# Chunked attention scores: the low-half pass of the queries over all 128 rows

## Chip, cores and metric

The kernel runs on one NeuronCore of a Trainium2 chip. The metric is device time in microseconds (us) of one execution, as the median of several runs. The engines are named as in the profile: PE is TensorE (PEld its weight loads), DVE is VectorE, ACT is ScalarE, POOL is GpSimd, SP is SyncE, which issues the DMAs here.

## The reference

One encoder layer on 1024 positions and 1024 channels in float32:

```
mod   = silu(c) @ w_ada + b_ada                     # six rows of shift, scale, gate
h     = rmsnorm(x) * (1 + scale) + shift
proj  = h @ w_in                                    # latents, rotary key, q/k/v of the chunked heads
o_mla = latent attention   (8 heads, chunk-causal, 96 channels a head)
o_ca  = chunk_attention(rmsnorm(cq), rmsnorm(ck), cv, rel_bias)    # 8 heads of 64 channels
x     = x + g_a * (concat(o_mla, o_ca) @ w_out)
x     = x + g_m * (silu(gate) * val @ w_down)       # gate, val = causal conv of (h2 @ w_up)
```

In `chunk_attention` each chunk of 64 queries sees the keys of its own chunk and of the 8 chunks before it; the scores are scaled by 64 ** -0.5, a clipped relative-position bias is added, and a softmax follows. The change is in the product of queries and keys of these heads.

## The kernel before

**Precision.** Matmuls run on float32r operands. A float32 value is split into a high half (the value rounded to float32r) and a low half (what is left), and a product is the sum of high by high, high by low and low by high (`gemm3`, L151 to L156).

**Chunked heads.** Two heads (o = 0 and 1) share a page: rows 0 to 63 of a tile hold the 64 channels of the even head, rows 64 to 127 those of the odd one, and 512 positions lie along the columns. `ca_pages` makes the pages of a pair p (0 to 3) and a group g (0 or 1: the positions 0 to 511 or 512 to 1023). Four transposes on PE bring the normalized queries into PSUM (`page_psum`, L729). For each head, `qh[o]` holds the queries' high half twice: in the head's own rows (ACT, L755) and, copied by POOL (L757), in the other 64 rows. `kk[:, o]` holds the keys' high half in the head's own rows and their low half in the other rows (L761, L762). One matmul over 128 rows of `qh[o]` and `kk[:, o]` so gives high by high and high by low together. The queries' low half, `ql` (DVE, L756), is one tile for both heads, each head in its own 64 rows. The third product, low by high, is a second matmul over the head's own 64 rows alone.

**Score tiles.** A unit is one head of one group, with four tiles of 128 queries; `scores` (L797) runs the qh pass and then the ql pass into the same PSUM tile. Keys come in one segment for the tiles of group 0 (128 to 512 columns) and in two for those of group 1 (512 and 128, 384 and 256, and so on). After the scores, DVE adds the bias and takes the minimum (L818; the sign is turned, so that the minimum is what the softmax subtracts), ACT takes the exponential with its sum (L829), DVE the reciprocal (L831, L832), POOL and DVE write the probabilities as two float16 halves (L73, L851), SP transposes them by DMA (L863), and PE multiplies them by the values (L891). A unit's pages are made two tiles ahead of it.

**Latent heads.** They come after the chunked heads, with the same chain. Their queries' high and low halves have tiles of the tag Q2 too (`qk_page`), and their three score products run over 96 rows each (L803).

**Order.** The program is written as score tiles with filler work between them (`pace`): the other input projections (L154 to L156), the latents, the up projections. The order on each engine is planned at build time from priorities and data readiness; the scores have a higher priority than the fillers. A side job, `f_ada`, computes rows 2 to 4 of `mod`: 48 pieces of 128 by 512 of `w_ada` are loaded by SP (L446) and multiplied and summed on DVE (L458, L460), one step at a time among the fillers; each load is placed behind the SP instruction issued last, each step behind the last score minimum. The pieces, the running sum and later the raw tiles of `w_out` (`load_wo`, L699) share the buffers of the tag A.

**Memory.** A tag's `bufs` is the number of its tiles that exist at one time. `apg` and `at` are pools of the attention stage; `at` lies where the tiles of the starting stage lay.

Of the kernel before, what the change touches and what calls it, by code (L numbers as in the profile page):

```python
# [13 lines left out]
F32 = mybir.dt.float32  # L14
F32R = mybir.dt.float32r
# [7 lines left out]
MUL, ADD, SUB, MIN, MAX = ALU.mult, ALU.add, ALU.subtract, ALU.min, ALU.max  # L23

P = 128
# [39 lines left out]
def layer_kernel(ctx, tc, I, out):  # L65
    nc = tc.nc
    pe, act, dve, pool, sp = nc.tensor, nc.scalar, nc.vector, nc.gpsimd, nc.sync

    def f32(ap):
        return ap.bitcast(F32)  # L70
# [57 lines left out]
    apg = att_pg.__enter__()  # L128
# [13 lines left out]
        return apg.tile([P, 512], F32, name=name, tag="sq", bufs=2)  # L142

    def atile(name):
        return apg.tile([P, 512], F32, name=name, tag="A", bufs=5)

    def pgtile(shape, dt, name):
        return apg.tile(shape, dt, name=name, tag="pg", bufs=6)
# [133 lines left out]
    for d in range(ND):  # L282
        dd, half = divmod(d, 2)
# [6 lines left out]
        pt = ps.tile([P, 512], F32, name=f"p_ada{d}", tag="mm", bufs=2)  # L290
# [23 lines left out]
    at = att.__enter__()  # L314
# [121 lines left out]
    def f_ada():  # L436
        steps = [(m, n, k) for m in (2, 3, 4) for n in range(2) for k in range(ND)]
        wt = {}

        def load(i):  # L440
            if i < len(steps):
                m, n, k = steps[i]
                wt[i] = atile(f"aw{m}_{n}_{k}")
                c0 = m * D + n * 512
                with tc.issue_after(anchor["sp"]):
                    sp.dma_start(wt[i][:], I["w_ada"][k * P:(k + 1) * P, c0:c0 + 512])  # L446

        for i in range(3):
            load(i)
        yield 0  # L450
        yield 0
        for i, (m, n, k) in enumerate(steps):
            if k == 0:
                acc = atile(f"aacc{m}_{n}")
            load(i + 3)
            with tc.issue_after(anchor["dve"]):
                if k == 0:
                    dve.tensor_scalar(acc[:], wt[i][:], cs[:, 0:1], None, op0=MUL)  # L458
                else:
                    dve.scalar_tensor_tensor(acc[:], wt[i][:], cs[:, k:k + 1], acc[:], op0=MUL, op1=ADD)  # L460
            yield 0
            if k < ND - 1:
                continue
            yield 0
            pt = ps.tile([P, 512], F32, name=f"p_ada{m}_{n}", tag="mm", bufs=2)
            if m == 2:
                gate_bcast(pt[:], acc, m * D + n * 512, 512, qtile)
                g = qtile(f"gab{n}")
                act.activation(g[:], pt[:], AF.Copy)
                sp.dma_start(ga_d[:, n * 512:(n + 1) * 512], g[:])  # L470
            else:
                for j in range(4):
                    pe.matmul(pt[:, j:j + 1], acc[:, j * P:(j + 1) * P], ones[:, 0:1], start=True, stop=True)
                act.activation(modT[:, 3 if m == 3 else 2, 4 * n:4 * n + 4], pt[:, 0:4], AF.Copy)
            yield 0
        b = pk[:, C_B + 24:C_B + 40].rearrange("p (a b) -> p a b", a=2)
        dve.tensor_tensor(modT[:, 3, :], modT[:, 3, :], b[:, 0], op=ADD)
        dve.tensor_tensor(modT[:, 2, :], modT[:, 2, :], b[:, 1], op=ADD)
        dve.scalar_tensor_tensor(modT[:, 2, :], modT[:, 2, :], 1.0, pk[:, C_GM:C_GM + ND], op0=ADD, op1=MUL)
# [240 lines left out]


    def q2(name):
        return at.tile([P, 512], F32R, name=name, tag="Q2", bufs=6)

    def page_psum(src, name, rows, tag="T"):
        pt = ps.tile([P, 512], F32, name=f"{name}_ps", tag=tag, bufs=TB)
# [18 lines left out]
    def ca_pages(p, g):  # L745

        qn = qns[p, g]
        half = (slice(0, 64), slice(64, 128))
        pt = page_psum(lambda j: qn[:, j, 0:128], f"q{p}_{g}", P)
        if p == g == 0:  # L750
            pk_ = page_psum(lambda j: qn[:, j, 128:256], f"k{p}_{g}", P, "pv")
        qh = [q2(f"qh{p}_{g}_{o}") for o in range(2)]
        ql = q2(f"ql{p}_{g}")
        for o in range(2):
            act.activation(qh[o][half[o]], pt[half[o]], AF.Copy)  # L755
            dve.tensor_tensor(ql[half[o]], pt[half[o]], f32(qh[o][half[o]]), op=SUB)  # L756
            pool.tensor_copy(qh[o][half[1 - o]], f32(qh[o][half[o]]))  # L757
        pt = pk_ if p == g == 0 else page_psum(lambda j: qn[:, j, 128:256], f"k{p}_{g}", P)
        kk = at.tile([P, 2, 512], F32R, name=f"k{p}_{g}", tag="K", bufs=3)
        for o in range(2):  # L760
            act.activation(kk[half[o], o], pt[half[o]], AF.Copy, scale=gk_ca[half[o]])  # L761
            dve.scalar_tensor_tensor(kk[half[1 - o], o], pt[half[o]], gk_ca[half[o]], f32(kk[half[o], o]),  # L762
                                     op0=MUL, op1=SUB)
        return (qh, ql), kk

    class Unit:
# [7 lines left out]
        def scores(u, i):  # L774

            qpg, kpgs = u.pages()
            bias = u.bias() if u.band else None
            lo = max(0, i - 4) if u.band else 0
            n = (i - lo + 1) * P
# [3 lines left out]
            with tc.high_priority(offset=OFF_S):  # L783
                s = ps.tile([P, 1024], F32, name=f"s{nm}", tag="S", bufs=2)
                n0 = max(0, min(4, i + 1) - lo) * P
                n1 = n - n0
                c0 = 512 - n0 if n1 else 0
                segs = [(c0, lo * P, n0, 0)] if n0 else []
                if n1:
                    segs.append((512, max(lo, 4) * P - 512, n1, 1))  # L790
                q = slice((i % 4) * P, (i % 4 + 1) * P)
                rs_ = slice(u.base, u.base + u.rows)
                if u.band:
                    qh, ql = qpg
                    for a, rr in ((qh[u.odd], slice(0, P)), (ql, rs_)):
                        for c, ko, w, kh in segs:
                            last = pe.matmul(s[:, c:c + w], a[rr, q], kpgs[kh][rr, u.odd, ko:ko + w],  # L797
                                             start=(a is not ql), stop=(a is ql))
                else:
                    for a in range(2):  # L800
                        for c, ko, w, kh in segs:
                            for b in range(2 - a):
                                last = pe.matmul(s[:, c:c + w], qpg[a][rs_, q], kpgs[kh][rs_, b, ko:ko + w],  # L803
                                                 start=(a == 0 and b == 0), stop=(a == 1))
                trail.append(last.ins)
                sv = s[:, c0:c0 + n]
                m = cst.tile([P, 1], F32, name=f"m{nm}", tag="m", bufs=4)
                if u.band:
                    if i >= 4:
                        dve.memset(sv[64:128, 0:64], BIG)  # L810
                    w = min(n, 256)
                    if n > 256:
                        m0 = cst.tile([P, 1], F32, name=f"m0{nm}", tag="m0", bufs=4)
                        dve.tensor_reduce(m0[:], sv[:, :n - 256], axis=AX.X, op=MIN)
                        init = m0[:]
                    else:
                        init = 3e38
                    anchor["dve"] = dve.tensor_tensor_reduce(sv[:, n - w:n], sv[:, n - w:n], bias[:, 256 - w:256], 1.0, init,  # L818
                                             ADD, MIN, accum_out=m[:]).ins
                else:  # L820
                    dve.memset(sv[0:64, n - 64:n], BIG)
                    anchor["dve"] = dve.tensor_reduce(m[:], sv, axis=AX.X, op=MIN).ins  # L822
                short = n <= (640 if u.band else 512)
                pieces = [(0, n)] if short else [(0, 512), (512, n)]
                if n <= 640:
                    pr = at.tile([P, 640], F32, name=f"P{nm}", tag="P", bufs=P_BUFS)
                else:
                    pr = pgtile([P, 1024], F32, f"P{nm}")
                act.activation(pr[:, :n], sv, AF.Exp, bias=m[:], scale=-1.0, accum_out=rsum[:, 0:1])  # L829
            with tc.high_priority(offset=OFF_P):  # L830
                dve.reciprocal(ri[:], rsum[:, 0:1])  # L831
                dve.tensor_scalar(ri[:], ri[:], PSCALE, None, op0=MUL)  # L832
                for x, (p0, p1) in enumerate(pieces):
                    w = p1 - p0
# [33 lines left out]
        def values(u, i):  # L868
# [17 lines left out]
            with tc.high_priority(offset=OFF_V):  # L886
                for x, (_, j, c, w, mov) in enumerate(todo):
                    dst = u.pv[:, c:c + w]
                    if w > P:
                        dst = dst.rearrange("p (a b) -> p a b", a=2)  # L890
                    last = pe.matmul(dst, u.vst(j), mov, start=(x == 0), stop=(x == len(todo) - 1),  # L891
                                     skip_group_check=True)
                trail.append(last.ins)
                if i % 4 == 3:
# [9 lines left out]
                    else:  # L904
                        anchor["om"] = sp.dma_start(u.dst_d[r0, u.g * 512:(u.g + 1) * 512], dst[r0]).ins
            return 56 * sum(w // P for _, _, _, w, _ in todo)

    cnt = [0]
    pair = [0]
# [112 lines left out]
    for n in range(len(tiles) + DEPTH):  # L1022
        if n < len(tiles):
            u, i = tiles[n]
# [9 lines left out]
        if n >= DEPTH:  # L1034
            u, i = tiles[n - DEPTH]
# [140 lines left out]
    for t in range(NT):  # L1176
        pt = ps2.tile([P, 1024], F32, name=f"op{t}", tag="op", bufs=3)
# [36 lines left out]
    for k in range(4):  # L1214
# [4 lines left out]
        for q, wl, wh in rows0:  # L1219
            product(q[:, 512:], wl, "b12", add=k > 0, ks=[k], skip=True)  # L1220
            last = product(q[:, 512:], wh, "b22", add=True, ks=[k])
# [226 lines left out]
    def load(o, i):  # L1448
        inorder("sp", sp.dma_start, o, i)
# [199 lines left out]
```

## Time and profile before

| | |
|---|---|
| runs | 1331.33, 1333.23, 1334.52 us; median 1333.23 us |
| profiled execution, first to last instruction | 1332.7 us |
| mean granted PE clock | 0.958 |
| busy: PE, PEld, DVE, ACT, POOL | 91%, 75%, 82%, 47%, 43% |
| instructions | 18710 |

The profile lists no time of the profiled execution beside its span; the span is 0.5 us below the median of the runs. A busy PE is not a PE at its peak, since the ends of matmuls are modelled; the starts of matmuls and of weight loads are what the steps are read from. In a timeline row the columns are start, duration, engine, line, operation, tiles (out<-in), shape and count, and in brackets the idle time of that engine before it with what ended it; "issue" means that nothing which the profile shows was waited for. The shape of a PE row begins with rows*columns of the weights. The row of a stretch gives its length and, for each engine, busy time and instructions, then the granted clock, the DMA share and GB/s.

### The profile page before, as it was taken

Reading aid. Unit: us, or ns where it says so; the run is one execution under the profiler, and the core shown is the slowest. Engines: PE = TensorE matmul, PEld = TensorE weight load, DVE = VectorE, ACT = ScalarE, POOL = GpSimd, SP = SyncE. Lnnn points to the kernel's source line nnn. Section 1 sums busy time; section 2 is a strip of 40 time slices with the busy share of each in tenths; the row PEclk is TensorE's granted clock in tenths of the full one; section 3 lists DMA queues with packets and bytes.
Section 4 is the critical chain, followed back from the end, with each engine's and each line's share of the span. In section 5 each row is a group of like instructions: output and inputs, shape, how many; then the busy total and the mean of one; then the engine's idle time right before and its main releaser. Section 6 shows DMA issues by size and latency. Waiting matters only on the chain.

```text
span 1332.7 us, 18710 instructions
## 1 busy us (share of the span) xinstructions
PE 1212.8 (91%) x6168; PEld 997.1 (75%) x6168; DVE 1088.7 (82%) x1928; ACT 622.3 (47%) x1132; POOL 572.3 (43%) x610
## 2 busy tenths in 40 slices
PE   3899999989667798888889999999999998999998
PEld 3888878868555576666677888888888886888886
DVE  6979898877589967894779888898889986687667
ACT  5454654445555545553366444444443444443331
POOL 5476773675675633354615445444444541000000
PEclk9899999989878798997999999999999998999999
DMA  8416768766123685879702333333333336943441
GB/s 321 144 55 156 164 143 197 150 151 138 35 72 70 119 172 122 152 164 326 275 16 79 106 124 111 122 116 108 113 106 132 111 119 221 393 151 114 132 159 63
DMA packets 223689, 190.57 MB, mean 143 GB/s; under 512 B 148708, under 2 KB 166884, under 8 KB 223592
## 3 DMA queue, kind: packets, MB, share of 16 engines
q1 hardware_dynamic: 223592, 189.38, 50.3%
q8 instruction: 48, 0.79, 0.3%
q14 instruction: 49, 0.40, 0.1%
HBM read 117.24 MB, written 37.49 MB: 116 GB/s over the span
## 4 chain that ended last, share of the span: by engine, by line
PE 48%; DVE 3%; DMA 2%; issue 1%; ACT 1%; POOL 0%; SPq 0%; POOLq 0%; DVEq 0%
PE p L1125 10%; PE p L1126 10%; PE p L1127 10%; PE dnA_P L1460 2%; PE dnA_P L1461 2%; PE dnA_P L1462 2%; PE dnB_P L1461 1%; PE dnB_P L1460 1%; PE dnB_P L1462 1%; PE dnA L1461 1%; PE dnA L1460 1%; PE dnA L1462 1%; PE dnB L1461 1%; PE dnB L1462 1%; PE dnB L1460 1%
## 5 line engine op out<-in xcount | busy, mean ns | idle before, releaser
L77 ACT ACTIVATE dnP<-dnr 128x1024 fp32r<-128x1024 f32 x73 | 77.4, 1064 | 117.5 <-PE dnA_P L1462 46.4
L1434 DVE TENSOR_TENSOR dnP<-dnr,dnP 128x1024 fp32r<-128x1024 f32 x72 | 87.9, 1224 | 52.7 <-ACT dnP L77 47.7
L73 POOL TENSOR_SCALAR hlm<-Pm,rim 128x512 f16<-128x512 f32 (+2 forms) x96 | 65.4, 691 | 77.5 <-DVE rim L832 32.0
L84 POOL TENSOR_TENSOR wf<-wu,wf 128x512 fp32r<-128x512 f32 x22 | 39.8, 1808 | 118.2 <-ACT wf L77 118.2
L1296 DVE SCALAR_TENSOR_TENSOR u<-c,cvp,u 128x1023 f32<-128x1023 f32 x44 | 58.6, 1372 | 27.8 <-ACT u L1295 27.8
L84 POOL TENSOR_TENSOR wb<-wu,wb 128x512 fp32r<-128x512 f32 x22 | 42.2, 1920 | 75.0 <-ACT wb L77 59.6
L73 POOL TENSOR_SCALAR hlc<-Pc,ric 128x640 f16<-128x640 f32 (+2 forms) x64 | 48.0, 753 | 54.5 <-DVE ric L832 25.8
L851 DVE SCALAR_TENSOR_TENSOR hlm<-Pm,rim,hlm 128x512 f16<-128x512 f32 (+2 forms) x96 | 65.9, 696 | 5.5 <-POOL hlm L73 5.2
L829 ACT ACTIVATE Pc<-sc,mc 128x640 f32<-128x640 f32 (+2 forms) x64 | 42.2, 660 | 55.2 <-DVE mc L818 26.1
L891 PE MATMUL pvm<-PTm,vt 128*128 128x256 f16 (+1 forms) x320 | 47.7, 302 | 22.1 <-DMA PTm<-hlm 14.2
L829 ACT ACTIVATE Pm<-sm,mm 128x128 f32<-128x128 f32 (+3 forms) x64 | 47.1, 738 | 37.7 <-DVE mm L822 21.2
L1295 ACT ACTIVATE u<-c,cvp 128x1024 f32<-128x1024 f32 x44 | 52.4, 1238 | 26.0 <-DVE c L1394 18.0
L1297 DVE SCALAR_TENSOR_TENSOR u<-c,cvp,u 128x1022 f32<-128x1022 f32 x44 | 61.7, 1442 | 0.0
L891 PEld LDWEIGHTS <-vt 128*128 128x128 f16 x320 | 33.1, 111 | 37.0 <-issue 21.6
L77 ACT ACTIVATE wc<-ws 128x512 fp32r<-128x512 f32 x21 | 13.3, 632 | 91.9 <-DVE ws L1144 86.1
L154 PE MATMUL ipq<-wq_s,hT 128*128 128x256 f32 x192 | 55.7, 290 | 0.0
L156 PE MATMUL ipq<-wq_s,hT 128*128 128x256 f32 x192 | 55.4, 288 | 0.0
L155 PE MATMUL ipq<-wq_s,hT 128*128 128x256 f32 x192 | 55.1, 287 | 0.0
L851 DVE SCALAR_TENSOR_TENSOR hlc<-Pc,ric,hlc 128x640 f16<-128x640 f32 (+2 forms) x64 | 49.2, 774 | 6.8 <-POOL hlc L73 6.7
L1461 PE MATMUL dnA_P<-dnP 128*128 128x512 f32 x132 | 51.3, 389 | 0.0
L1462 PE MATMUL dnA_P<-dnP 128*128 128x512 f32 x132 | 51.3, 389 | 0.0
L1460 PE MATMUL dnA_P<-dnP 128*128 128x512 f32 x132 | 51.2, 389 | 0.0
(442 smaller groups left out, 4413.7 us busy)
## 6 DMA issues: line engine op xcount, KB each, us to landing
wu<-w_up SPq DMA_DIRECT2D x44, 512.0 KB, 3.5
dnr<-g_d SPq DMA_DIRECT2D x73, 256.0 KB, 2.8
aw<-w_ada SPq DMA_DIRECT2D x48, 256.0 KB, 3.4
g_d<-u SPq DMA_DIRECT2D x22, 512.0 KB, 3.0
dnr<-w_down SPq DMA_DIRECT2D x44, 256.0 KB, 5.4
adaw<-w_ada_a SPq DMA_DIRECT2D x16, 512.0 KB, 6.0
x<-x SPq DMA_DIRECT2D x16, 512.0 KB, 9.8
g_d<-gs SPq DMA_DIRECT2D x22, 256.0 KB, 2.8
```

Source lines behind the costliest of these rows:

```text
L73: pool.tensor_scalar(o, i, s, 1.0, op0=MUL, op1=MUL)
L77: act.activation(o, i, AF.Copy)
L84: (pool if eng == "p" else dve).tensor_tensor(o, i, f32(hi), op=SUB)
L829: act.activation(pr[:, :n], sv, AF.Exp, bias=m[:], scale=-1.0, accum_out=rsum[:, 0:1])
L851: dve.scalar_tensor_tensor(hl[:, w:2 * w], pp, ri[:], hl[:, :w], op0=MUL, op1=SUB)
L1125: pe.matmul(pt, sh, pg[:, 0], start=(k == 0 and not add), stop=False, skip_group_check=skip)
L1126: pe.matmul(pt, sh, pg[:, 1], start=False, stop=False, skip_group_check=skip)
L1127: last = pe.matmul(pt, sl, pg[:, 0], start=False, stop=(k == 3), skip_group_check=skip)
L1434: r = f(*a, **k)
L1460: pe.matmul(pt, sh, w[:, 0, 0], start=start, stop=False, skip_group_check=add)
L1461: pe.matmul(pt, sh, w[:, 1, 0], start=False, stop=False, skip_group_check=add)
L1462: pe.matmul(pt, sl, w[:, 0, 0], start=False, stop=stop, skip_group_check=add)
```

## The change

The low halves of the queries get tiles of their own, three for the whole run (`qlow`). The other 64 rows of each are set to zero once by POOL. `qlow[0]` holds the even head's low half, `qlow[1]` and `qlow[2]` that of the odd head for the two groups. The ql pass of the scores then takes all 128 rows of the query tile and of `kk[:, o]`; the zero rows meet the keys' low half and add nothing. For the memory, the tag Q2 goes from 6 tiles to 4 (a page of the chunked heads takes two of them in place of three) and the tag A from 5 to 4, with two loads of `f_ada` ahead in place of three.

```diff
--- before.py
+++ after.py
@@ -142,7 +142,7 @@
         return apg.tile([P, 512], F32, name=name, tag="sq", bufs=2)
 
     def atile(name):
-        return apg.tile([P, 512], F32, name=name, tag="A", bufs=5)
+        return apg.tile([P, 512], F32, name=name, tag="A", bufs=4)
 
     def pgtile(shape, dt, name):
         return apg.tile(shape, dt, name=name, tag="pg", bufs=6)
@@ -445,14 +445,14 @@
                 with tc.issue_after(anchor["sp"]):
                     sp.dma_start(wt[i][:], I["w_ada"][k * P:(k + 1) * P, c0:c0 + 512])
 
-        for i in range(3):
+        for i in range(2):
             load(i)
         yield 0
         yield 0
         for i, (m, n, k) in enumerate(steps):
             if k == 0:
                 acc = atile(f"aacc{m}_{n}")
-            load(i + 3)
+            load(i + 2)
             with tc.issue_after(anchor["dve"]):
                 if k == 0:
                     dve.tensor_scalar(acc[:], wt[i][:], cs[:, 0:1], None, op0=MUL)
@@ -720,7 +720,7 @@
 
 
     def q2(name):
-        return at.tile([P, 512], F32R, name=name, tag="Q2", bufs=6)
+        return at.tile([P, 512], F32R, name=name, tag="Q2", bufs=4)
 
     def page_psum(src, name, rows, tag="T"):
         pt = ps.tile([P, 512], F32, name=f"{name}_ps", tag=tag, bufs=TB)
@@ -750,10 +750,10 @@
         if p == g == 0:
             pk_ = page_psum(lambda j: qn[:, j, 128:256], f"k{p}_{g}", P, "pv")
         qh = [q2(f"qh{p}_{g}_{o}") for o in range(2)]
-        ql = q2(f"ql{p}_{g}")
+        ql = qlow[0], qlow[1 + g]
         for o in range(2):
             act.activation(qh[o][half[o]], pt[half[o]], AF.Copy)
-            dve.tensor_tensor(ql[half[o]], pt[half[o]], f32(qh[o][half[o]]), op=SUB)
+            dve.tensor_tensor(ql[o][half[o]], pt[half[o]], f32(qh[o][half[o]]), op=SUB)
             pool.tensor_copy(qh[o][half[1 - o]], f32(qh[o][half[o]]))
         pt = pk_ if p == g == 0 else page_psum(lambda j: qn[:, j, 128:256], f"k{p}_{g}", P)
         kk = at.tile([P, 2, 512], F32R, name=f"k{p}_{g}", tag="K", bufs=3)
@@ -792,10 +792,10 @@
                 rs_ = slice(u.base, u.base + u.rows)
                 if u.band:
                     qh, ql = qpg
-                    for a, rr in ((qh[u.odd], slice(0, P)), (ql, rs_)):
+                    for x, a in enumerate((qh[u.odd], ql[u.odd])):
                         for c, ko, w, kh in segs:
-                            last = pe.matmul(s[:, c:c + w], a[rr, q], kpgs[kh][rr, u.odd, ko:ko + w],
-                                             start=(a is not ql), stop=(a is ql))
+                            last = pe.matmul(s[:, c:c + w], a[:, q], kpgs[kh][:, u.odd, ko:ko + w],
+                                             start=(x == 0), stop=(x == 1))
                 else:
                     for a in range(2):
                         for c, ko, w, kh in segs:
@@ -904,6 +904,11 @@
                     else:
                         anchor["om"] = sp.dma_start(u.dst_d[r0, u.g * 512:(u.g + 1) * 512], dst[r0]).ins
             return 56 * sum(w // P for _, _, _, w, _ in todo)
+
+    qlow = [at.tile([P, 512], F32R, name=f"qlow{n}") for n in range(3)]
+    for n, t in enumerate(qlow):
+        zero = slice(64, 128) if n == 0 else slice(0, 64)
+        pool.memset(f32(t[zero]), 0.0)
 
     cnt = [0]
     pair = [0]
```

## The prediction

> **What bounds the kernel now.** I read the page's engine line first, then busy time by stretches over the stage of the chunked heads, then the order of instructions around single score tiles, and last the waits of VectorE (DVE) in that stage.
>
> ```profile
> PE 1212.8 (91%) x6168; PEld 997.1 (75%) x6168; DVE 1088.7 (82%) x1928; ACT 622.3 (47%) x1132; POOL 572.3 (43%) x610
> ```
> ```profile
> L797 PEld LDWEIGHTS sc<-k,ql x96: 182/183/285, 86.4 to 325.5; 64*128 64x128 f32 x96
> L797 PE MATMUL sc<-k,ql x96: 217/382/792, 86.4 to 325.6; 64*128 64x128 f32 x24, 64*128 64x256 f32 x24, 64*128 64x384 f32 x24, 64*128 64x512 f32 x24
> ...
>   issue: 10.8, 49
> ```
> ```profile
> core 0: us, PE busy (x) PEld busy (x) DVE busy (x) ACT busy (x) POOL busy (x), PEclk, DMA share, GB/s
> 82.00:330.00 248.00, 235.13 (x1616) 203.11 (x1615) 214.32 (x600) 128.42 (x328) 152.58 (x207) 0.98 0.68 152
> ```
> ```profile
> 82.00:100.00 18.00, 17.71 (x132) 16.12 (x130) 13.61 (x44) 10.24 (x27) 12.05 (x19) 1.00 0.34 100
> 100.00:140.00 40.00, 38.12 (x285) 33.58 (x285) 38.02 (x118) 17.29 (x38) 24.46 (x26) 1.00 0.73 167
> 140.00:180.00 40.00, 39.42 (x288) 34.14 (x285) 35.86 (x100) 28.36 (x71) 30.34 (x36) 1.00 0.57 130
> 180.00:220.00 40.00, 36.49 (x259) 31.30 (x259) 35.01 (x100) 19.47 (x45) 19.69 (x24) 0.96 0.88 191
> 220.00:260.00 40.00, 40.00 (x308) 35.73 (x306) 36.06 (x93) 18.02 (x43) 22.80 (x27) 1.00 0.76 159
> 260.00:300.00 40.00, 34.35 (x185) 27.30 (x184) 31.61 (x80) 19.00 (x55) 27.21 (x46) 0.91 0.62 154
> 300.00:330.00 30.00, 29.06 (x172) 24.94 (x171) 24.14 (x70) 16.04 (x51) 16.03 (x32) 1.00 0.64 132
> ```
>
> The changed pass (ql) runs from 86 to 326 us. There TensorE (PE) is busy 235.1 of 248.0 us and DVE 214.3. In four stretches (82 to 100, 140 to 180, 220 to 260, 300 to 330; 128 of the 248 us) PE has next to no idle time and DVE has some: these are bound by PE. From 100 to 140 DVE is as full as PE, and in 180 to 220 and 260 to 300 PE waits 3.5 and 5.7 us. So PE time taken out is worth its price in about half of the stage.
>
> Now one tile of two segments (256 and 384 keys), among filler matmuls of an input projection:
>
> ```profile
> 132.84 0.28 PE L154 MATMUL ipq<-wq_s,hT 128*128 128x256 f32 x1
> 132.84 0.19 PEld L155 LDWEIGHTS ipq<-wq_s,hT 128*128 128x128 f32 x1
> 132.96 0.28 PE L155 MATMUL ipq<-wq_s,hT 128*128 128x256 f32 x1
> ...
> 133.56 0.31 PEld L797 LDWEIGHTS sc<-k,qh 128*128 128x128 f32 x2
> 133.68 0.46 PE L797 MATMUL sc<-k,qh 128*128 128x256 f32 x2
> 134.07 0.29 PEld L797 LDWEIGHTS sc<-k,ql 64*128 64x128 f32 x2 [0.19 <-issue]
> 134.07 0.55 PE L797 MATMUL sc<-k,ql 64*128 64x256 f32 x2
> 134.55 0.19 PEld L155 LDWEIGHTS ipq<-wq_s,hT 128*128 128x128 f32 x1 [0.19 <-issue]
> 134.55 0.39 PE L155 MATMUL ipq<-wq_s,hT 128*128 128x256 f32 x1
> ...
> 134.78 0.28 PE L156 MATMUL ipq<-wq_s,hT 128*128 128x256 f32 x1
> ```
>
> Between fillers, whose operands have 128 rows, a weight load begins 0.12 us ahead of its matmul, under the matmul before it, and 256 columns take a step of 0.12 us. At the change to 64 rows (134.07) and at the change back (134.55) the load path stands still for 0.19 us with nothing to wait for, and the load then begins at the same moment as its matmul: nothing covers it. One segment does the same:
>
> ```profile
> 158.72 0.34 PE L797 MATMUL sc<-k,qh 128*128 128x384 f32 x1
> 158.98 0.44 PE L797 MATMUL sc<-k,ql 64*128 64x384 f32 x1
> 159.35 0.39 PE L156 MATMUL ipq<-wq_s,hT 128*128 128x256 f32 x1
> 159.57 0.28 PE L154 MATMUL ipq<-wq_s,hT 128*128 128x256 f32 x1
> ```
>
> Whether the rows make the pause, or the low half, the latent heads show; their low pass keeps its 96 rows:
>
> ```profile
> 588.09 0.77 PEld L803 LDWEIGHTS sm<-mk,mq_1h 96*128 96x128 f32 x4
> 588.78 0.30 PEld L803 LDWEIGHTS sm<-mk,mq_1l 96*128 96x128 f32 x2
> ```
>
> No pause stands between these rows, and the low load starts under the high pass. So the pause belongs to the 64 rows.
>
> **The change part by part.** *The ql pass on 128 rows.* The number of matmuls, their columns and the loads stay (96 and 96). What goes is the pair of pauses with the uncovered loads. In the first tile, 133.68 to 134.78 is 1.10 us for five matmuls; at 0.12 us for 256 columns and 0.18 for 384 (0.12 x 384/256, an estimate) they need 3 x 0.12 + 2 x 0.18 = 0.72. In the second, 158.72 to 159.57 is 0.85 us where 2 x 0.18 + 0.12 = 0.48 are needed. So 0.38 and 0.37 us a tile, one price for both kinds. There are 4 pairs of heads x 2 groups x 2 heads x 4 tiles = 64 tiles: 64 x 0.38 = 24 us of PE time.
>
> A page of the Trainium skill speaks against this: "TensorE: Matmul & The Clock Gate", Part 3, The mechanism, says that a weight load overlaps a running matmul only when the row groups differ. By that rule a ql load over all rows would stay uncovered, and only the pause would go. The filler rows above disagree: at 132.84 a load on all 128 rows begins with a matmul on all 128 rows and is over before the next step but one.
>
> What of the 24 us comes off the end? The floor is what DVE waits for PE itself today:
>
> ```profile
> DVE sc L810 <- PE sc L797: 6.0, 9, 1.2
> ...
> DVE aacc L460 <- DMA aw<-w_ada: 3.1, 4, 1.7
> ...
> DVE m0c L814 <- PE sc L797: 1.1, 4, 0.3
> ...
> DVE sc L818 <- PE sc L797: 0.3, 1, 0.3
> ```
>
> That is 6.0 + 1.1 + 0.3 = 7.4 us. The ceiling is DVE's work at its fullest share, 38.02/40 = 95%: 214.3/0.95 = 225.5, so 248.0 - 225.5 = 22.5 us. I choose between them by the stretches: the four that PE bounds hold half of the stage, so half of the 24, 12 us, counts in full; of the other 12 I take a quarter, 3 us, since DVE or a wait is as late there. Gain: **15 us**. After 330 us the latent heads follow in the same order, so an earlier start carries through to the end; what is late next in the stage is DVE.
>
> *Tag A from five tiles to four, two loads ahead in place of three.* Each of the 48 pieces of the conditioning weights is put into SyncE's queue one step later, behind the transposes of the probabilities that lie between. DVE runs in order: what queues behind a late piece is the score minimum, the reciprocal and the low halves of the probabilities, and behind those the transposes and the value matmuls.
>
> ```profile
> L460 DVE SCALAR_TENSOR_TENSOR aacc<-aw,cs,aacc x42: 725/752/1469, 116.8 to 303.3; 128x512 f32<-128x512 f32 x42
> ```
> ```profile
> aw<-w_ada SPq DMA_DIRECT2D x48, 256.0 KB, 3.4
> ```
>
> The steps are (303.3 - 116.8)/47 = 4.0 us apart on the mean, so the lead goes from about 12 to 8 us against a landing of 3.4: covered on the mean, but the steps come in bunches, and with three ahead DVE waits already 3.1 us in 4 places. Bounds: nothing (a buffer less gives no gain), and a whole landing at each of those four, 13.6 us. I take as much again as today, **3 us**, nearest to the measured wait. The same tag holds the output projection's raw weights, the last of which are split here:
>
> ```profile
> 605.11 0.68 DVE L84 TENSOR_TENSOR wo<-wor,wo 128x512 fp32r<-128x512 f32 x1
> ```
> ```profile
> 638.26 0.80 PE op L156
> ```
>
> The matmuls that use them start about 32 us after that, so one load that comes a landing later is hidden; without that cover it would cost one landing, about 3 us.
>
> *Three zeroed half tiles on GpSimd (POOL), once.*
>
> ```profile
> L101 POOL MEMSET ones<- 128x128 f32 x1 | 0.2, 204 | 0.0
> ...
> L103 POOL MEMSET nhalf<- 128x1 f32 x1 | 0.1, 98 | 0.0
> ```
> ```profile
> 85.01 1.27 POOL L757 CAST qh<-qh 64x512 fp32r<-64x512 f32 x2
> ```
>
> From these, 512 columns are 98 + 4 x 106 = 0.5 us, and no more than a copy of that form, 0.6. Three are 1.5 to 1.9 us. They lie either under earlier POOL gaps (nothing) or just ahead of the first copies, which the first scores at 86 us need (1.9). I take **0.5**.
>
> *At nothing:* Q2 from six tiles to four: a page pair of the chunked heads took three and takes two, so two pairs fit as before; the latent heads keep two units instead of three, and the unit two back has sent its last scores to PE before the transposes that the new copies wait for. The single qlow tile of the even head is written after transposes that stand behind its last readers in PE's order; without that cover a page would wait for part of a tile. The low-half subtractions keep number and form.
>
> Sum against the profiled execution: 1332.7 - 15 + 3 + 0.5 = 1321.2 us of span. The median of the runs, 1333.23, lies 0.5 above that span, so **1322 us**. About 0.2%, 2.7 us, is what a measurement of this kernel can tell from no change.
>
> **The rivals.** *DVE takes over at once.* Only the 7.4 us come off: 1333.2 - 7.4 + 3.5 = 1329. For it: DVE is 95% full from 100 to 140 us. Against: in 58 us of the stage (82 to 100, 260 to 300) DVE is busy less than 80%. *All of it comes off.* 22.5 us with no added waits: 1311. Against it: both engines would stand at about 95%, which today only one stretch in seven shows.
>
> *Slower: DVE stands behind the conditioning weights.* Every landing that DVE waits out in full costs up to 3.4 us, since the scores' minimum queues behind it. Six of them (20 us) eat the 15 us and bring a loss over 2.7; eight (27 us) give 1333.2 - 15 + 27 = 1345. For it: waits with three ahead, and SyncE's queue in which the loads stand behind transposes. Against: the mean lead, and that the planner places a step by when its piece should be there.
>
> *The pause stays* because it belongs to the low pass and not to its rows: nothing gained, the 3.5 us paid, 1337. Against it: the latent heads' rows. *Loads stay uncovered on equal rows*: a load waits for the matmul that holds the same rows, so of 0.38 us a tile the two loads' share stays. The filler step after the change back is 134.78 - 134.55 = 0.23 in place of 0.12, so 0.11 each, and 0.38 - 0.22 = 0.16 goes: 64 x 0.16 = 10 us, of which 15/24 count: 6, so 1333.2 - 6 + 3.5 = 1331. The covered loads of the filler rows speak against it. It is what the rule of the Trainium skill above would bring.
>
> **How the numbers follow.** The forecast (1314 to 1326) 0.50; DVE at once (1326 to 1331) 0.17; all of it (below 1314) 0.08; slower by the weights (above 1336) 0.15; the pause stays (1333 to 1337) 0.07; loads uncovered (about 1331) 0.03. The range 1311 to 1337 leaves out some 0.04 below and most of the slower rival, 0.12, above. Faster by over 0.2%, below 1330.5: 0.50 + 0.08 + most of the second, 0.15, and a part of the last, 0.02: 0.75. Within it: the remaining 0.03 of these and half of "the pause stays", together 0.07. Slower: the rest, 0.18.
>
> **What would show it.** Right: ql rows read 128*128, their load starts under the qh matmul, line 797's idle time by issue (10.8 us) is nearly gone, its last start moves from 325.5 to 310 to 314 us, and DVE's share in that stage rises from 86% to about 92%. The waits of aacc for aw stay under 7 us. Wrong: the pauses are still there, or the stage ends as late as before with PE idle more and DVE waiting for aw or ACT; or the stage ends earlier and the time comes back between 330 and 640 us.

## The result, and the profile after

The changed kernel takes 1326.57 us (median of 11 runs, 1321.14 to 1331.36) against 1333.23 us before (11 runs): ratio 0.9951, 95% interval 0.9935 to 0.9967, so 6.5 us off, between 4.4 and 8.7. The forecast was 1322 us, 11 us off. The profiled execution spans 1325.1 us, 7.6 less than that of before.

The passes of the score line in the changed kernel (duration min/median/max in ns, first and last start in us), then what its engine waited for:

```profile
L797 PEld LDWEIGHTS sc<-k,qlow x96: 187/188/333, 86.8 to 323.0; 128*128 128x128 f32 x96
...
  ACT Pc L829: 22.6, 19
  issue: 0.2, 1
```

The low pass has 128 rows, and the idle time "by issue" went from 10.8 to 0.2 us. In its place stands a wait of 22.6 us (weight loads and matmuls counted together, so much of it stands there twice) for ACT's exponentials, which have to read a score buffer before the next scores go into it; it was 7.4 us. The stretch of the chunked heads:

```profile
82.00:330.00 248.00, 223.91 (x1666) 208.95 (x1665) 214.95 (x604) 133.07 (x342) 160.31 (x227) 0.98 0.67 154
```

PE is busy 223.9 us in place of 235.1, though more of its instructions fall into the stretch (1666 against 1616). DVE does what it did. A tile of two segments (256 and 384 keys), as in the prediction, from the changed kernel's order of instructions (rows of PE and its weight loads alone):

```profile
131.72 0.56 PE L797 MATMUL sc<-k,qh 128*128 128x256 f32 x2 [1.46 <-ACT Pc L829]
131.95 0.36 PEld L797 LDWEIGHTS sc<-k,qlow 128*128 128x128 f32 x2
132.12 0.46 PE L797 MATMUL sc<-k,qlow 128*128 128x256 f32 x2
132.24 0.19 PEld L156 LDWEIGHTS ipq<-wq_s,hT 128*128 128x128 f32 x1
132.42 0.28 PE L156 MATMUL ipq<-wq_s,hT 128*128 128x256 f32 x1
...
132.54 0.28 PE L154 MATMUL ipq<-wq_s,hT 128*128 128x256 f32 x1
```

The load of qlow begins 0.17 us ahead of its matmul and under the qh pass, and the filler's load under the qlow pass. From 131.72 to 132.54 the tile takes 0.82 us where it took 1.10. But the first row says what came instead: PE had stood 1.46 us before this tile, waiting for ACT. What DVE and PE waited for in the stage, in the changed kernel (us in total, times, longest):

```profile
DVE aacc L460 <- DMA aw<-w_ada: 4.0, 5, 1.8
...
DVE sc L810 <- PE sc L797: 1.5, 2, 1.1
DVE m0c L814 <- PE sc L797: 1.5, 3, 0.6
...
DVE sc L818 <- PE sc L797: 1.1, 1, 1.1
```
```profile
PE pvc L891 <- DMA PTc<-hlc: 10.2, 8, 2.5
PE sc L797 <- ACT Pc L829: 10.0, 8, 2.7
```

PE's own waits for the transposed probabilities (PTc) and for the exponentials were shorter before:

```profile
PE pvc L891 <- DMA PTc<-hlc: 4.5, 5, 1.9
PE sc L797 <- ACT Pc L829: 3.1, 3, 1.8
```

DVE waits 4.1 us for scores, where it waited 7.4.

### The profile page after: what moved, and what is told of

It is laid out like the page before. It is cut to its first block, busy times and chain, and to the rows that moved or that the text cites. A ratio compares the mean times of both kernels' runs of the same rounds, so it can differ in the third digit from the quotient of the medians.

```text
span 1325.1 us, 18721 instructions
## 1 busy us (share of the span) xinstructions
PE 1191.0 (90%) x6168; PEld 992.2 (75%) x6168; DVE 1086.5 (82%) x1928; ACT 623.6 (47%) x1132; POOL 580.7 (44%) x613
## 4 chain that ended last, share of the span: by engine, by line
PE 50%; DVE 4%; DMA 3%; issue 2%; ACT 1%; POOL 1%; SPq 0%; POOLq 0%; DVEq 0%; ACTq 0%
PE p L1130 10%; PE p L1131 10%; PE p L1132 10%; PE dnA_P L1465 2%; PE dnA_P L1467 2%; PE dnA_P L1466 2%; DMA PTm<-hlm 2%; PE dnB_P L1467 2%; PE dnB_P L1465 2%; PE dnB_P L1466 2%; PE dnA L1465 1%; PE dnA L1466 1%; PE dnA L1467 1%; PE sm L803 1%; PE dnB L1467 1%
## 5 line engine op out<-in xcount | busy, mean ns | idle before, releaser
L73 POOL TENSOR_SCALAR hlm<-Pm,rim 128x512 f16<-128x512 f32 (+2 forms) x96 | 68.8, 728 | 85.7 <-DVE rim L832 45.6
L1301 DVE SCALAR_TENSOR_TENSOR u<-c,cvp,u 128x1023 f32<-128x1023 f32 x44 | 55.8, 1309 | 27.8 <-ACT u L1300 23.7
L73 POOL TENSOR_SCALAR hlc<-Pc,ric 128x640 f16<-128x640 f32 (+2 forms) x64 | 48.8, 764 | 47.0 <-DVE ric L832 17.8
L1302 DVE SCALAR_TENSOR_TENSOR u<-c,cvp,u 128x1022 f32<-128x1022 f32 x44 | 55.5, 1300 | 0.0
```

Of the source, the lines that this page charges most:

```text
L73: pool.tensor_scalar(o, i, s, 1.0, op0=MUL, op1=MUL)
```

## The experiments

Twelve kernels ran. Differences in us below are 1333 x (1 - ratio), with the 95% interval of the ratio against runs of the kernel before on the same chip.

### The rows alone, in the order of before

```diff
-  for a, rr in ((qh[u.odd], slice(0, P)), (ql, rs_)):
+  for a, rr in ((qh[u.odd], slice(0, P)), (ql, slice(0, P))):
```

> The kernel before, with one edit: the ql pass takes all 128 rows of the shared tile ql, in which the other 64 rows hold the other head's low half, so the third product also adds that head's low half times this head's key low half. No buffer changes, no zeroing, and the planned order on every engine is that of the kernel before, instruction for instruction. Theory A (the two pauses a tile go, and what is not realised is lost to score tiles that now wait for ACT to read the score buffer): idle by issue at line 797 falls from 10.8 to under 1 us, PE's busy time in the stage by 10 us or more, waits of the score pass for Pc rise by 5 us or more, and the time falls by 6 to 12 us (ratio 0.991 to 0.9955). Theory B (the gain of the changed kernel comes from the new order that the planner found with other buffers): within 3 us of before. Theory C (the smaller tags cost about 3.5 us, as the prediction has it): 3 to 4 us faster than the changed kernel.

1330.03 us, ratio 0.9973 [0.9948, 0.9999]: 3.6 us faster [0.1, 6.9]. The instructions of every engine stand in the same order as before, so its profile can be laid on that of before:

```profile
82.00:330.00 248.00, 219.29 (x1613) 203.04 (x1612) 213.55 (x599) 127.68 (x327) 155.03 (x207) 0.97 0.66 152
```
```profile
PE pvc L891 <- DMA PTc<-hlc: 15.2, 11, 3.6
PE sc L797 <- ACT Pc L829: 6.2, 6, 2.5
```
```profile
DVE sc L810 <- PE sc L797: 2.6, 2, 1.7
...
DVE sc L818 <- PE sc L797: 0.9, 1, 0.9
```

The pauses are gone, and PE is busy 15.8 us less with nearly the same work. The first tile that the prediction priced (256 and 384 keys) now takes 0.75 us, 129.85 to 130.60, where it took 1.10:

```profile
129.85 0.50 PE L797 MATMUL sc<-k,qh 128*128 128x256 f32 x2
130.19 0.46 PE L797 MATMUL sc<-k,ql 128*128 128x256 f32 x2
130.48 0.28 PE L155 MATMUL ipq<-wq_s,hT 128*128 128x256 f32 x1
130.60 0.28 PE L156 MATMUL ipq<-wq_s,hT 128*128 128x256 f32 x1
```

The second one takes 0.47 us (155.46 to 155.93) where it took 0.85. The waits for transposes rose by 10.7 us and those for exponentials by 3.1: together 13.8 of the 15.8 us. What theory A said of the pauses and of new waits came, but the larger wait is that of the value matmuls for the transposes, and the gain stayed below its 6 us. DVE's waits for scores fell by 3.9 us (7.4 to 3.5), about as much as the run gained. The profiles do not show that the one is the other. The last matmul of the latents (mp), which stands near the end of this stage, starts only 0.4 us earlier than before, at a granted clock of 0.97 in the stage against 0.98. First before, then this run:

```profile
L156 PE MATMUL mp<-wm_h,hT x64: 345/353/548, 264.5 to 335.9; 128*128 128x416 f32 x64
```
```profile
L156 PE MATMUL mp<-wm_h,hT x64: 346/353/549, 262.1 to 335.5; 128*128 128x416 f32 x64
```

This profiled execution is 3.9 us shorter than that of before (1328.8 against 1332.7 us), and most of that comes after the stage. Theory B (within 3 us) is not excluded by the interval, theory C (faster than the changed kernel) fell.

### The smaller tags alone

```diff
-  return apg.tile([P, 512], F32, name=name, tag="A", bufs=5)      # and range(3), load(i + 3)
+  return apg.tile([P, 512], F32, name=name, tag="A", bufs=4)      # and range(2), load(i + 2)
```

> The kernel before with tag A at 4 tiles and two loads ahead alone. Theory A and C: 1 to 4 us slower (ratio 1.001 to 1.003), aacc waits for aw 4 to 7 us against 3.1. Theory B: the new order alone moves the time by more than 3 us, to either side.

1330.39 us, ratio 0.9981 [0.9959, 1.0002]: 2.5 us faster [-0.3, 5.5], where theories A and C had it slower; the "more than 3 us" of theory B is not reached by the median either. The wait that the prediction priced did grow, from 3.1 to 5.2 us, within the 4 to 7 that were expected:

```profile
DVE aacc L460 <- DMA aw<-w_ada: 5.2, 6, 2.2
```

The other tag, with the low tile in a tag of its own:

```diff
-  return at.tile([P, 512], F32R, name=name, tag="Q2", bufs=6)
+  return at.tile([P, 512], F32R, name=name, tag="Q2", bufs=4)
-  ql = q2(f"ql{p}_{g}")
+  ql = at.tile([P, 512], F32R, name=f"ql{p}_{g}", tag="QL", bufs=2)
```

> The kernel before with tag Q2 at 4 tiles and ql in a tag of its own with two tiles, so that only the latent heads have fewer pages. Theory A and C: within 1.5 us of before. Theory B: over 3 us to either side, through the new order.

1328.48 us, ratio 0.9962 [0.9940, 0.9983]: 5.1 us faster [2.3, 8.0], against "within 1.5". Less memory does no work, but with each of these edits the planner writes a new order: of the 6168 places in PE's order, 1208 hold another matmul with the smaller tag A, and 480 with the smaller Q2. That the order is what moves the time is likely, but it is not shown apart from the buffers, and only the second interval lies clear of zero. This is theory B's part of the truth.

### Tag A at five again, with two low tiles

```diff
-  ql = qlow[0], qlow[1 + g]                    # three low tiles, tag A at 4, two loads ahead
+  ql = qlow[0], qlow[1]                        # two low tiles, tag A at 5, three loads ahead
```

> The changed kernel with tag A at 5 tiles and three loads ahead again, and the memory for it from the third low tile: the odd heads of both groups share one. Theory C: 2 to 4 us faster than the changed kernel, so 9 to 11 us faster than before (ratio 0.992 to 0.993). Theory A without C: within 2 us of the changed kernel. If the single odd tile makes DVE wait for the scores of the unit before, DVE's line 756 shows a wait for PE line 797, and the gain is smaller than the changed kernel's 6.7 us.

1322.99 us, ratio 0.9923 [0.9893, 0.9952], from 6 runs: 10.3 us faster than before [6.4, 14.3]. The single odd tile costs nothing that shows: DVE's line 756 waits for no scores. It is the time that theory C named, but not by its cause, since DVE waits longer for the conditioning weights than in the changed kernel (4.0 us):

```profile
DVE aacc L460 <- DMA aw<-w_ada: 5.9, 6, 1.4
```

The interval overlaps that of the changed kernel.

### The new order with 64 rows

```diff
-  last = pe.matmul(s[:, c:c + w], a[:, q], kpgs[kh][:, u.odd, ko:ko + w],
+  rr = slice(0, P) if x == 0 else rs_
+  last = pe.matmul(s[:, c:c + w], a[rr, q], kpgs[kh][rr, u.odd, ko:ko + w],
```

> The changed kernel with the ql pass on the head's own 64 rows again; the order on every engine is that of the changed kernel. With the kernel before, the changed kernel and the rows alone it makes a square of two orders by two row counts. Theory D (the new order gains by itself, the rows little): 3 to 7 us faster than before, the last filler matmul of the latents (mp) starts at 329 to 333 us against 335.9 before and 328.4 after. Theory E (the new order pays only where the pauses are gone): within 2 us of before, mp ends at 335 to 338 us; the rows are then worth 6 to 7 us in the new order and about 3 in the old. Theory F (PE bounds the new order): slower than before by 3 us or more, mp ends after 340 us.

1331.06 us, ratio 0.9989 [0.9974, 1.0004]: 1.5 us faster than before [-0.5, 3.5]. Theory E's numbers come nearest: the order with its buffers is worth little alone, and the rows 6.5 - 1.5 = 5.0 us in it (2.9 to either side), though mp starts last at 339.4 us where that theory had 335 to 338. Its last latent matmul, with that of the changed kernel:

```profile
L156 PE MATMUL mp<-wm_h,hT x64: 346/353/548, 267.1 to 339.4; 128*128 128x416 f32 x64
```
```profile
L156 PE MATMUL mp<-wm_h,hT x64: 345/351/548, 257.8 to 328.4; 128*128 128x416 f32 x64
```

The stage ends 11 us earlier with the rows, but only about half of that is left in the time. Part of the 11 us can be the clock, which was 0.95 in the stage of this execution and 0.98 in that of the changed kernel:

```profile
82.00:330.00 248.00, 236.89 (x1600) 205.43 (x1599) 210.02 (x587) 126.58 (x318) 150.34 (x206) 0.95 0.65 149
```

In the profile of before, around 195 us, the granted clock is 0.50, and a filler matmul of 256 columns takes a step of 0.21 us there in place of 0.12. So 0.03 of 248 us can be worth up to 7 us of PE time (an estimate). Part of the lead also goes again later. With the two profiles laid on each other matmul by matmul, the lead is 9.2 us where the changed kernel stands at 542 us and 5.0 at 552. In between, PE waits 2.8 us for a transpose, and the granted clock of the changed kernel is 0.50, against 1.00 with 64 rows at the same matmuls:

```profile
545.00:551.50 6.50, 5.95 (x23) 4.73 (x24) 2.29 (x8) 1.20 (x3) 2.19 (x4) 0.50 0.62 152
```

In this order, with 64 rows, DVE waits most for scores (the edit moves the lines below it by one):

```profile
DVE m0c L815 <- PE sc L798: 6.9, 8, 2.4
DVE sc L811 <- PE sc L798: 4.8, 7, 2.0
DVE sc L819 <- PE sc L798: 2.3, 4, 1.2
```

That is 14.0 us, of which the changed kernel keeps 4.1.

### More pauses

```diff
-  for a, rr in ((qh[u.odd], slice(0, P)), (ql, rs_)):
-      for c, ko, w, kh in segs:
+  for c, ko, w, kh in segs:
+      for a, rr in ((qh[u.odd], slice(0, P)), (ql, rs_)):
```

> The kernel before with the qh and ql pass of each segment next to each other, so that a tile of two segments changes between 128 and 64 rows four times in place of twice; the orders of DVE, ACT, POOL and SP stay. That is 32 tiles x 0.38 us = 12 us more PE time. Theory G (PE stands at the edge: time added costs in full, time taken out gives little, since DVE or the transposes are as late): 8 to 12 us slower (ratio 1.006 to 1.009). Theory H (PE has slack in this order, as little is gained when the pauses go): under 4 us slower. By the prediction's own reading (half of the stage is bound by PE): 6 us slower.

1339.17 us, ratio 1.0045 [1.0028, 1.0062]: 6.0 us slower [3.7, 8.3] for some 12 us of added PE time. Half of it costs, as the prediction's own reading had it; G asked for 8 to 12 and H for under 4, which the interval touches at its two ends. DVE's waits for scores doubled, from 7.4 to 14.7 us:

```profile
DVE sc L810 <- PE sc L797: 11.5, 14, 1.8
DVE m0c L814 <- PE sc L797: 2.9, 5, 1.8
DVE sc L818 <- PE sc L797: 0.3, 1, 0.3
```

So 7.3 us more waiting, 6.0 us more time. As with the rows alone, the time moved by about as much as these waits did. The stage itself does not tell the same in both directions: here the last latent matmul starts 7.8 us later than before (343.7 against 335.9), with the rows alone 0.4 us earlier.

### DVE relieved

```diff
-  dve.scalar_tensor_tensor(acc[:], wt[i][:], cs[:, k:k + 1], acc[:], op0=MUL, op1=ADD)
+  dve.scalar_tensor_tensor(acc[:, :8], wt[i][:, :8], cs[:, k:k + 1], acc[:, :8], op0=MUL, op1=ADD)
```

> The kernel before with the accumulation of the conditioning rows on 8 of the 512 columns alone (the rest of the sums is left out): 42 DVE instructions of 0.88 us become some 0.15 us, 30 us of DVE work less in the stage; the order is planned anew. If PE bounds the stage before: under 5 us faster than before. If DVE bounds it: 12 us or more.

1325.30 us, ratio 0.9948 [0.9924, 0.9973]: 6.9 us faster [3.6, 10.1], between the two forecasts.

> The same with the ql pass over all 128 rows of the shared tile; the order on every engine is that of the run before it with 64 rows. Theory G (DVE is what is late once the pauses are gone): with DVE relieved the rows are worth 10 to 20 us against the same kernel with 64 rows. Rival (the chain score, exponential, transpose, value is late, whatever DVE has to do): the rows are worth 0 to 5 us here too, and PE waits for the transposes (PTc) as long as in the run with the rows alone, about 15 us.

1322.87 us, ratio 0.9933 [0.9910, 0.9955]: 2.0 us faster than the same with 64 rows, by the two ratios (4.4 to either side). The forecast of theory G (10 to 20) fell: with 18 to 20 us of DVE work less in the stage PE's time still does not come through.

```profile
82.00:330.00 248.00, 223.56 (x1662) 208.43 (x1660) 195.89 (x603) 132.63 (x344) 154.62 (x235) 0.98 0.67 156
```

Here PE is busy 90% and DVE 79%, and neither is full. The rival's time came, but not its wait: PE waits 5.6 us for PTc here, not 15. What DVE waits for is spread over DMA, POOL, ACT and PE, and no one of them stands out:

```profile
DVE aacc L460 <- DMA aw<-w_ada: 9.2, 11, 1.3
DVE hlc L851 <- POOL hlc L73: 7.3, 8, 2.2
DVE k L762 <- ACT k L761: 6.6, 3, 2.9
DVE ric L831 <- ACT Pc L829: 5.9, 9, 1.0
...
DVE sc L810 <- PE sc L797: 2.7, 3, 2.2
...
DVE m0c L814 <- PE sc L797: 1.8, 1, 1.8
```

Waits for scores were 6.9 us in the run with 64 rows and are 5.1 here (with 0.6 at line 818): 1.8 us less.

### A step of DVE put on POOL

```diff
-  dve.tensor_scalar(ri[:], ri[:], PSCALE, None, op0=MUL)
+  pool.tensor_scalar(ri[:], ri[:], PSCALE, 1.0, op0=MUL, op1=MUL)
```

> The changed kernel with two low tiles and tag A at 5 (as in the run before with that), and the factor 2**15 put on the reciprocals by POOL in place of DVE: 128 DVE instructions of 0.15 us (19 us, half of them in the stage of the chunked heads) become 128 of about 0.2 us on POOL, which is busy 44%. The question is a version better than both. If DVE is what is late: 1313 to 1320 us. If the chain between the engines is late: no faster than 1323, since POOL's step takes the place of DVE's in it, or slower.

> The changed kernel with that step on POOL alone. If DVE's work is late: 4 to 9 us faster than the changed kernel (1318 to 1323). If the chain is late: within 2 us of it, or slower.

> The kernel before with that step on POOL. If PE is late there as the prediction has it for half of the stage: 1 to 4 us faster than before, less than the same step gives on the changed kernel. If the chain is late: within 2 us or slower.

On the kernel with two low tiles: 1329.27 us, ratio 0.9977 [0.9961, 0.9994]. On the changed kernel: 1328.35 us, 0.9973 [0.9958, 0.9989]. On the kernel before: 1324.71 us, 0.9945 [0.9926, 0.9963]. On the kernel before the step gains 7.3 us [4.9, 9.9], where 1 to 4 were the most that was expected, so neither forecast came there. On the other two it costs time: 7.2 us on the kernel with two low tiles (4.5 to either side) and 2.9 on the changed kernel (3.0 to either side), as the forecasts for a late chain allowed. A cause for these three is not settled: each has an order of its own, as the kernels with the smaller tags had, whose times moved by 2.5 and 5.1 us.

The last kernel takes the rows into the fastest of these orders:

```diff
-  for a, rr in ((qh[u.odd], slice(0, P)), (ql, rs_)):            # the kernel of the run before
+  for a, rr in ((qh[u.odd], slice(0, P)), (ql, slice(0, P))):
```

> The kernel before with the factor 2**15 on POOL (the run before, 1324.71 us) and the ql pass over all 128 rows of the shared tile ql, which adds the product of the other head's low halves of queries and keys; the order on every engine is that of the run before. A third pair of row counts in one order, and a version that may beat the changed kernel. Theory I (the rows are worth what DVE waits for scores of PE, not the PE time): in the run with 64 rows DVE waits 3.2 + 3.0 + 1.2 + 0.8 = 8.2 us for line 797 of PE between 82 and 330 us; some 3 to 5 of it go, so 3 to 5 us faster, 1319.5 to 1321.5 us. Theory A of the prediction (60% of 24 us of PE time): 10 us or more faster, under 1315 us. Rival (the rows pay in no order but by chance): within 2 us of 1324.7.

1322.40 us, ratio 0.9926 [0.9899, 0.9952], from 6 runs: 2.6 us less than the run before by the two ratios, not quite theory I's 3 to 5, far from A's 10. The interval of the difference (4.3 to either side) takes in the rival's 2 us too. DVE's waits for scores went from 8.2 to 2.5 us. (The 64 rows that are added multiply the other head's query low half by this head's key low half, as in the rows alone.)

The four pairs in one order side by side (in us, from 64 to 128 rows; PE busy and granted clock between 82 and 330 us; waits of DVE for scores as read above):

| order | PE busy | DVE's waits for scores | time gained by the rows | last latent matmul | granted clock |
|---|---|---|---|---|---|
| before | 235.1 to 219.3 | 7.4 to 3.5 | 3.6 | 335.9 to 335.5 | 0.98 to 0.97 |
| changed kernel | 236.9 to 223.9 | 14.0 to 4.1 | 5.0 | 339.4 to 328.4 | 0.95 to 0.98 |
| DVE relieved | 240.3 to 223.6 | 6.9 to 5.1 | 2.0 | 328.1 to 325.6 | 0.99 to 0.98 |
| scale on POOL | 239.0 to 222.9 | 8.2 to 2.5 | 2.6 | 329.5 to 327.1 | 0.98 to 0.98 |

The second column is read in a fixed stretch, into which 66 more matmuls fall in the second pair with 128 rows (1600 and 1666). For the same work, from the first score to the last latent matmul, PE is busy 15.5, 24.4, 17.6 and 17.8 us less; of the 24.4, up to 7 can be the clock.

The mean gain is 3.3 us; with half widths of 3.4, 2.9, 4.4 and 4.3 us taken as independent, it is known to 1.9. It is far nearer to the third column than to the second, where each pair gives 13 to 17 us. The kernel with two low tiles (1322.99 us) and the last one (1322.40 us) have lower medians than the changed kernel, but their intervals overlap its own, so neither is shown to be better.

## Why the prediction was right

**The pause.** Right. The pause belongs to the change between 128 and 64 rows: with the rows alone changed it vanished, with twice the changes in the two-segment tiles the idle time by issue rose from 10.8 to 14.7 us and 6 us were lost. The Trainium skill, "TensorEngine Tiling (Array Packing)", Key Properties, says that a change of the tiling mode drains TensorE; the rows of before agree, with 0.19 us of idle load path at each change, if 64 rows count as another mode than 128, which no row names.

**Loads on equal rows.** The rival is ruled out, as its chance of 0.03 had it: in the changed kernel the qlow load at 131.95 begins under the qh pass on the same 128 rows. The sentence of the Trainium skill, "TensorE: Matmul & The Clock Gate", Part 3, The mechanism, by which a load overlaps a running matmul only on other row groups does not hold here as it stands.

**24 us of PE time.** About right. The two tiles that were priced at 0.38 and 0.37 us take 0.35 and 0.38 us less with the rows alone. Over the same work PE's busy time fell by 15.5 to 17.8 us in the three pairs whose clocks differ by 0.01 at most. The busy time does not hold the pauses in full, so it can't settle the rest of the 24.

**15 of the 24 us come off.** This is the step that was mis-sized. The rows are worth about 3, in the changed kernel's order 5. The fault lies in the way from the stretches to the gain: I counted the stretches where PE has no idle time as bound by PE in full. They are full, but in them the chain of scores, minimum, exponential, reciprocal, probabilities and transposes was close behind, so that PE, set free, stood before a score buffer or before PTc (13.8 us more with the rows alone). The floor that I had written down, what DVE waits for PE itself (7.4 us), was the better estimate: in all four pairs the median gain is below such waits, and the part of them that went was 0.9 to 2.2 times what was gained. So the first rival, DVE at once, had the nearer number. Its mechanism is not shown: with 18 to 20 us of DVE's work gone, the rows were worth no more (2.0 us, 4.4 to either side). What PE waits for when it is set free is the chain between the engines; which link of it is late is open.

**Tag A, 3 us.** Not borne out: the tag alone came out 2.5 us faster [-0.3, 5.5]. The wait of aacc grew as priced (3.1 to 4.0 us in the changed kernel), but something else outweighed it, most likely the new order. The slower rival, DVE behind the weights, needed six full landings; five waits of 4.0 us in all came.

**The zeroed tiles, 0.5 us.**

```profile
L911 POOL MEMSET qlow<- 64x512 f32 x3 | 1.5, 521 | 0.1
```

The three take 1.5 us as worked out, and the first scores start 0.5 us later (86.7 against 86.2). That this is their doing is not shown: with the same three tiles, in the new order with 64 rows, the first scores start at 86.3 us, and with none, in the rows alone, at 85.6.

**The sum.** 15 - 3.5 was 11; it was 5 for the rows and 1.5 [-0.5, 3.5] for order and buffers. Two misses partly cancelled: too much gain, and a cost where none came. That the time falls by over 0.2%, and not by the whole 24 us, was right. The size was not the forecast's: 1326.6 us lies in the range that the first rival was given (1326 to 1331, chance 0.17) and not in the forecast's own (1314 to 1326). That it lies between 1311 and 1337 says little for the sum, since most of the rivals do too. Of the signs named, the stage's last score starts at 323.0 us, not 310 to 314, and DVE's share stayed at 87% where 92% were forecast: both said that the gain was smaller before any run did. The sign of a gain that comes back after 330 us did not show against before: the last latent matmul starts 7.5 us earlier (335.9 to 328.4), and the span is 7.6 us shorter.

## What to carry to other kernels

When an engine without idle time is sped up, don't multiply the time saved by the share of the stretches in which it is full; read what the next engine in the chain waits for from it, and take that as the most that comes off. It was so in the medians of all four pairs here; no run tests it on another kernel. A full engine and the chain beside it can be late together, and then time added cost half here, and busy time taken out gave about a fifth (3.3 of 13 to 17 us). Where the order is planned at build time, test an edit in one order (here a shared tile left the order as it was), since a changed buffer count alone moved this kernel by 2.5 us [-0.3, 5.5] in one run and by 5.1 [2.3, 8.0] in another. And before two single profiles are compared, compare the granted clocks of the stretch: a pair at 0.95 and 0.98 showed 11 us where 5 were in the times.

## What the runs showed that I had not expected

A pair of changes, 128 to 64 rows and back, costs 0.35 to 0.38 us of TensorE time around one score tile. The rows show the load path idle for 0.19 us twice, and two weight loads that begin with their matmuls; these lie partly under other work, so they do not add up to the price. The latent heads' passes over 96 rows show no such pause. And two kernels with the same order on every engine can differ in the granted clock of a stretch, 0.95 and 0.98 over the stage and 1.00 and 0.50 around 545 us, which is enough to make a gain look twice its size in one stage and to take it back in the next. What lowers the clock in one execution and not in the other was not tried.
